# A decoder trunk on one core: its instructions ordered by the scheduler's timeline model in place of its default model

## The chip, the core and the metric

The kernel runs on one core of one Trainium2 chip. A core has five engines that each work through their own list of instructions in order: TensorE (PE in the profile, with weight loads shown as PEld), VectorE (DVE), ScalarE (ACT), GpSimd (POOL) and SyncE (SP). They meet only at semaphores. The metric is the device time of one execution in microseconds (us). The kernel before took 4318.94 us, the median of 3 runs (4314.97 to 4319.62).

## The reference

One layer of a hybrid decoder over 1024 tokens of width 1024, in float32:

```
h  = RMSNorm(x);  z = h @ W_in            # one projection, 77 tiles of 128 columns and 2 blocks for v
x += W_out( sum_b sigmoid(gate_b) * (mixer_b(z_b) @ P_b) )   # b: mLSTM, Mamba-2 SSD, forgetting attention
x += PEER(RMSNorm(x))
x += sigmoid(RMSNorm(x) @ W_g) * (p @ W_p);  out = RMSNorm(x)
```

PEER is the part that matters most here. For each token, 8 heads choose 16 experts each out of 16384 (two top-16 searches over 128 keys, then a top-16 of their sums). An expert is one row `u` and one row `v` of width 1024: `out = sum over the 128 chosen of softmax(score) * gelu(u . x) * v`.

## The kernel before

The tokens are split into two halves of 512, and each half into 4 blocks of 128 tokens. The stages, in the order in which the code is written and with the times that the trace shows (us):

- 0 to 1080: the mixer of half 0 (`mixer`), its output projection (`mixer_out`), and the expert search (`route_keys`: 16 projections, each followed by top-16 searches on DVE).
- 1080 to 1300: `route` of half 0, a chain of small DVE instructions for each of 4 blocks (top-16 at L891 to L895, selections at L933 to L943, the row numbers `ii` at L980). In between run the norm, the small per-head rows (`small_rows`, L355 to L443) and the first projections of the mixer of half 1.
- 1300 to 2330: the mixer of half 1. Beside it, `experts_in` fetches the 512 groups of `u` rows of half 0: POOL issues a gather of 128 rows (L1014, one row for each token, 512 KB), DVE multiplies them with the tokens and sums (L1027, a "row operation" in what follows). Five buffers hold gathered rows here, so POOL is at most five gathers ahead of DVE.
- 2330 to 2690: `mixer_out`, `route_keys` and `route` of half 1, and the first build of a weight table (below).
- 2690 to 4130: `experts_out`. The `v` rows are not gathered for the first 6 blocks. Instead the kernel reads the whole table `peer_v` and multiplies it with a table `W` of weights (token by expert, mostly zero). The 128 expert columns are taken in chunks of 43, 43 and 42, in two passes of three blocks: 6 chunks. For one column, SP loads 512 KB (`vr`, L1170, 4 buffers) and PE does 6 products that are two matmuls each in the trace (L1174, "a step" of 12 matmuls: 3 blocks by 2 halves of the width). While PE works through chunk n, the `W` of chunk n+1 is built by `scatter`: 48 times DVE makes one-hot tiles (`A8`, `B8` at L1091, two `A8` buffers, and the scaled `Bs` at L1103, two buffers), PE multiplies them (L1070, 24 small matmuls, "a small product") and ACT copies the result into `W` (L1072). The same loop feeds the row operations of half 1 (L1027, then L1044 for the last two blocks).
- 4130 to 4314: the gate of the per-layer input, the last norm, and the output.

All matmuls of the projections take weights split in two parts: SP loads `raw` (L191), ACT casts it to `whi` (L182), DVE forms `wlo` (L183), and PE does three matmuls for each of 8 slices (L214; L329 for the blocks of v). `raw`, `whi` and `wlo` have two buffers each.

The kernel is written with a tile framework. The code names the engine of every instruction; a scheduler then orders each engine's list. It plays the program through a model of the machine: whenever an engine of the model is free, it takes the earliest-written instruction that is ready in the model at that time. The order that results is fixed in the program; on the chip nothing is reordered. In `experts_out` DVE is exempt (its instructions stay as written); PE and ACT are not:

```
    with tc.manual_schedule(engines={mybir.EngineType.DVE}):
        end = experts_out(vp, W, blocks, gen, then, last())
```

## Time and profile before

| | |
|---|---|
| runs of the kernel (median of 3) | 4318.94 us |
| the profiled execution: time, span | 4315.76 us, 4314.0 us |
| PE busy | 3987.3 us, 92% of the span |
| DVE busy | 3297.0 us, 76% |
| POOL busy | 1726.7 us, 40% |
| ACT busy | 1179.5 us, 27% |
| data moved by DMA | 1018.30 MB, 236 GB/s over the span |

A share over the whole span mixes stages with different limits, so the stages are read one by one. Matmuls are pipelined: the durations of single matmuls overlap, and the busy time of a stretch is less than their sum.

### The profile page before, as it was taken

What the parts mean: (1) busy time and instruction counts of PE and PEld (TensorE: products, weight loads), DVE (VectorE), ACT (ScalarE), POOL (GpSimd) and SP (SyncE); (2) the same over time, 40 slices, a digit from 0 to 9 for tenths busy, and PEclk for the clock granted to TensorE, in tenths of its full rate; (3) what the DMA queues carried; (4) which work ended last, traced back from release to release, by engine and by line L of the source; (5) the groups of instructions that cost most, each with busy time, mean ns of one, the idle gap of its engine ahead of it and who ended that gap; (6) DMA issues with size and microseconds to landing.
All of it is one profiled execution on the core that took longest, in us unless ns stands there. A gap on an engine that the chain in (4) does not pass through costs nothing. (4 is left out here: it accounts for less than half of the span.)

```text
span 4314.0 us, 55488 instructions
## 1 busy us (share of the span) xinstructions
PE 3987.3 (92%) x20506; PEld 2494.4 (58%) x20506; DVE 3297.0 (76%) x6607; ACT 1179.5 (27%) x2194; POOL 1726.7 (40%) x1299
## 2 busy tenths in 40 slices
PE   8999999999788988989978798999999999998987
PEld 5777687777466755655744573544445444443455
DVE  6333245648998877788887799998899899997855
ACT  3343334533325502422521410211111111110023
POOL 0000000000036676565364001677777666777620
PEclk9999999999899997899989799999999999999998
DMA  2212122233258898788687124999999999999962
GB/s 91 99 56 76 46 93 71 77 126 122 78 173 296 299 355 291 276 310 313 217 298 282 59 96 149 335 357 361 369 364 376 364 358 361 358 376 400 399 222 93
DMA packets 326081, 1018.30 MB, mean 236 GB/s; under 512 B 33584, under 2 KB 81072, under 8 KB 325552
## 3 DMA queue, kind: packets, MB, share of 16 engines
q0 software_dynamic: 184320, 671.17, 42.6%
q1 hardware_dynamic: 141488, 343.58, 22.5%
q8 instruction: 161, 2.64, 0.2%
q14 instruction: 112, 0.92, 0.1%
HBM read 992.84 MB, written 21.77 MB: 235 GB/s over the span
## 5 line engine op out<-in xcount | busy, mean ns | idle before, releaser
L1014 POOL DMA_INDIRECT ug<-in_peer_u_dram,ii x1024 | 1397.3, 1365 | 2248.3 <-DVE ii L980 1388.6
L1174 PE MATMUL pair<-vr,W 128*128 128x512 f32 x3072 | 1388.7, 603 | 24.5 <-DMA vr<-in_peer_v_dram 24.5
L1027 DVE CUSTOM_DVE_ANT_0 ug<-ug,hft 128x1024 f32<-128x1024 f32 x1024 | 1217.8, 1219 | 158.8 <-DMA ug<-in_peer_u_dram,ii 142.5
L1174 PEld LDWEIGHTS pair<-vr,W 128*128 128x128 f32 x3072 | 569.3, 192 | 661.5 <-issue 633.9
L214 PE MATMUL bank<-hi,wlo 128*128 128x512 f32 x1552 | 623.3, 402 | 24.8 <-DVE wlo L183 24.6
L214 PE MATMUL bank<-hi,whi 128*128 128x512 f32 x1552 | 632.4, 409 | 12.0 <-ACT hi L182 5.1
L214 PE MATMUL bank<-lo,whi 128*128 128x512 f32 x1552 | 624.5, 403 | 0.9 <-DVE lo L183 0.8
L182 ACT CAST whi<-raw 128x1024 fp32r<-128x1024 f32 (+1 forms) x276 | 282.2, 1023 | 1070.9 <-PE bank L214 633.5
L183 DVE TENSOR_TENSOR wlo<-raw,whi 128x1024 fp32r<-128x1024 f32 (+1 forms) x276 | 327.1, 1186 | 323.2 <-ACT whi L182 312.6
L1072 ACT COPY W<-bank 128x176 f32<-128x176 f32 x480 | 179.9, 484 | 950.1 <-PE bank L1070 901.3
L1014 POOL DMA_INDIRECT ug<-in_peer_v_dram,ii x256 | 325.5, 1271 | 184.1 <-DVE hft L1044 95.0
L1044 DVE SCALAR_TENSOR_TENSOR hft<-ug,gt,hft 128x1024 f32<-128x1024 f32 x254 | 325.9, 1283 | 52.8 <-DMA ug<-in_peer_v_dram,ii 47.4
L214 PEld LDWEIGHTS bank<-hi,whi 128*128 128x128 f32 x1552 | 296.0, 191 | 105.3 <-issue 26.4
L214 PEld LDWEIGHTS bank<-hi,wlo 128*128 128x128 f32 x1552 | 296.2, 191 | 102.2 <-DVE wlo L183 32.9
L214 PEld LDWEIGHTS bank<-lo,whi 128*128 128x128 f32 x1552 | 296.4, 191 | 72.4 <-issue 9.7
L1070 PEld LDWEIGHTS <-A 128*128 128x128 bf16 x6912 | 215.2, 98 | 198.7 <-issue 80.9
L1091 DVE TENSOR_TENSOR A<-iota,i 128x1024 bf16<-128x1024 bf16 x288 | 197.4, 686 | 41.8 <-PE bank L1070 36.7
L205 PE MATMUL bank<-Y,raw 128*128 128x512 f32 x384 | 183.4, 636 | 27.8 <-DVE p L840 16.3
L1070 PE MATMUL bank<-Bs,A 128*128 128x43 bf16 (+1 forms) x5760 | 182.3, 183 | 22.4 <-DVE Bs L1103 21.7
L1103 DVE TENSOR_TENSOR Bs<-B,w 128x1032 bf16<-128x1032 bf16 (+1 forms) x288 | 198.4, 689 | 5.9
L205 PEld LDWEIGHTS bank<-Y,raw 128*128 128x128 f32 x384 | 76.6, 203 | 128.5 <-issue 90.3
L329 PE MATMUL pair<-whi,hi 128*128 128x512 f32 x256 | 102.7, 402 | 10.7 <-ACT mg L332 7.6
(429 smaller groups left out, 4492.4 us busy)
## 6 DMA issues: line engine op xcount, KB each, us to landing
vr<-in_peer_v_dram SPq DMA_DIRECT2D x256, 512.0 KB
raw<-in_w_in_dram SPq DMA_DIRECT2D x154, 512.0 KB
raw<-in_w_br_dram SPq DMA_DIRECT2D x64, 512.0 KB
raw<-in_w_tm_dram SPq DMA_DIRECT2D x32, 512.0 KB
raw<-in_w_q_dram SPq DMA_DIRECT2D x32, 512.0 KB
ug<-in_peer_u_dram,ii POOLq DMA_INDIRECT x1024
raw<-in_w_pg_dram SPq DMA_DIRECT2D x14, 512.0 KB
Y<-in_xT_dram SPq DMA_DIRECT2D x16, 256.0 KB
```

Source lines behind the costliest of these rows:

```text
L182: A.copy(out=hi, in_=src)
L183: V.tensor_tensor(out=lo, in0=src, in1=hi, op=ALU.subtract)
L205: PE.matmul(o, lhsT=raw[:, k, :], rhs=X[k] if isinstance(X, list) else X[:, k, :], start=k == 0, stop=k == nk - 1)
L214: PE.matmul(o, lhsT=l[:, k, :], rhs=r[k], start=i == 0, stop=i == n - 1)
L1014: G.indirect_dma_start(out=x, out_offset=None, in_=table, in_offset=bass.IndirectOffsetOnAxis(ap=ii[:, s:s + 1], axis=0))
L1027: V.tensor_tensor_reduce(out=ug, in0=ug, in1=hft, scale=1.0, scalar=0.0, op0=ALU.mult, op1=ALU.add, accum_out=act[:, s:s + 1])
L1044: V.scalar_tensor_tensor(out=o, in0=vg, scalar=gt[:, s:s + 1], in1=o, op0=ALU.mult, op1=ALU.add)
L1070: PE.matmul(wp_[:, u, 0:nk], lhsT=A8[:, a, :, o], rhs=Bs[:, k, a, :, o], start=k == 0, stop=k == 2)
L1072: A.copy(out=W[k][:, 0:hi - lo, b * P + t:b * P + t + 8].rearrange("p i t -> p t i"), in_=wp_[:, :, lo:hi])
L1091: V.tensor_tensor(out=o, in0=iota2[:, k0:k0 + n].unsqueeze(1).to_broadcast([P, 4, n, 2]), in1=x[:, t:t + 8].rearrange("p (a o) -> p a o", ...
L1103: V.tensor_tensor(out=Bs, in0=B8.unsqueeze(1).to_broadcast([P, 3, 4, nk, 2]), in1=w3[:, t // 8].rearrange("p k (a o) -> p k a o", o=2).uns ...
L1174: PE.matmul(acc[b][d], lhsT=l[:, b * P:b * P + P], rhs=raw[:, d * T:d * T + T], start=i2 == 0, stop=i2 == P - 1)
```

## The change

One argument where the framework's context is opened:

```
-    with tile.TileContext(nc) as tc:
+    with tile.TileContext(nc, schedule_with_timeline_sim=True) as tc:
         tile_trunk(tc, *aps, o)
```

The code that emits the instructions is untouched. The scheduler works with the same rule, but "free" and "ready" are now those of another model, its timeline model. The instructions are the same (17470 matmuls on PE, 1280 gathers on POOL, 819 plain DMAs on SP as the program counts them), but for the activation tables that ACT loads, 70 after 91, and for some instructions that only wait. Their order differs on all engines; on POOL and SP only by a few places.

On DVE, between two weight tiles `wlo` of the last v projection of half 1's attention (`proj_tm`, L329). `ug` is a buffer of gathered rows; the `L1027 ISA ug` rows are the row operations and `L1027 ISA act` their sums; `mg`, `p_pk`, `ii` belong to `route`, `pts`, `p4`, `cl` to `small_rows`, `rw` to the norm of q and k. Before, whole from the one `wlo` to the other but for the rows left out, 9 row operations and 8 others:

```order
L183 TENSOR_TENSOR wlo_1293_8782<-raw_1291_8779,whi_1292_8781 128x1024
L938 TENSOR_TENSOR mg_997_6549<-mg_997_6549 128x8x128
L1027 ISA ug_1944_13526,act_1925_13472<-ug_1944_13526,hft_1926_13473 128x1024
L1027 ISA act_1925_13472 128x1
L941 TENSOR_REDUCE p_pk_1244_8445<-mg_997_6549 128x128
...
L980 SCALAR_TENSOR_TENSOR ii_1245_8447<-p_pk_1241_8434,p_pk_1244_8445 128x128
...
L242 TENSOR_SCALAR rw_1283_8729<-rw_1283_8729 128x64
L183 TENSOR_TENSOR wlo_1296_8812<-raw_1294_8809,whi_1295_8811 128x1024
```

Now, the same two tiles and some of the 86 row operations and 112 others between them:

```order
L183 TENSOR_TENSOR wlo_1293_8782<-raw_1291_8779,whi_1292_8781 128x1024
L1027 ISA ug0_1990_13664,act_1925_13472<-ug0_1990_13664,hft_1926_13473 128x1024
L1027 ISA act_1925_13472 128x1
L933 TENSOR_TENSOR mg_997_6549<-p_pb_1213_8241,sta_11_128 128x2048
L987 RECIPROCAL p_gs_1220_8264<-p_gs_1220_8264 128x8
L1027 ISA ug1_1991_13667,act_1925_13472<-ug1_1991_13667,hft_1926_13473 128x1024
...
L980 SCALAR_TENSOR_TENSOR ii_1218_8259<-p_pk_1214_8246,p_pk_1217_8257 128x128
...
L265 TENSOR_SCALAR rw_1282_8727<-pair2_70 128x64
...
L241 TENSOR_TENSOR rw_1283_8729<-rw_1283_8729,rw_1284_8730 128x64
L183 TENSOR_TENSOR wlo_1296_8812<-raw_1294_8809,whi_1295_8811 128x1024
```

Row operations moved forward, from behind the tile to ahead of it, and `route` of the third and fourth block, which before stood mostly ahead of the first of the two tiles, moved back behind it. Counted from the first block's row numbers (`ii`, L980) to `wlo_1296`, 26 row operations stood there before and 149 stand there now. Ahead of `wlo_1293` it was 17 and is 63, ahead of the tile that DVE makes at 1868 us in the trace, 301 and 474. The last of the 512 stood in `mixer_out`; now it stands beside the output products of the mLSTM branch, ahead of the SSD mixer.

On PE, at the end of the third of the six builds of `W` (the one that ends at 3108.8 us in the trace; every row `L1070` shown is the first of the 24 of its small product, `Bs` names the product, `W_2803` is the table in use, `W_3069` the one being built). Before:

```order
L1070 MATMUL bank0_66<-Bs_3375_22402,A8_3369_22355 128x42
...
L1174 MATMUL pair0_68<-vr_3381_22443,W_2803_18264 128x512 x2
L1174 MATMUL pair1_69<-vr_3381_22443,W_2803_18264 128x512 x2
L1174 MATMUL pair2_70<-vr_3381_22443,W_2803_18264 128x512 x2
L1070 MATMUL bank1_67<-Bs_3382_22451,A8_3376_22404 128x42
...
L1174 MATMUL pair0_68<-vr_3388_22492,W_2803_18264 128x512 x2
L1174 MATMUL pair1_69<-vr_3388_22492,W_2803_18264 128x512 x2
L1174 MATMUL pair2_70<-vr_3388_22492,W_2803_18264 128x512 x2
```

Now, with nothing of L1174 between the rows shown:

```order
L1174 MATMUL pair1_69<-vr_3429_22751,W_3069_20299 128x512 x2
L1070 MATMUL bank1_67<-Bs_3339_22154,A8_3337_22124 128x42
...
L1070 MATMUL bank0_66<-Bs_3375_22402,A8_3369_22355 128x42
...
L1070 MATMUL bank1_67<-Bs_3382_22451,A8_3376_22404 128x42
...
L1070 MATMUL bank0_66<-Bs_3399_22581,A8_3397_22551 128x42
...
L1174 MATMUL pair2_70<-vr_3406_22623,W_3069_20299 128x512 x2
```

Steps of L1174 moved ahead of small products, so that a build begins with pairs of small products with two steps or so behind each pair, and ends with a run of small products that has no step in it. Of the 48 small products of a build, the last 24, 10, 13, 8 and 12 (second to sixth build) now have only 8, 0, 6, 0 and 0 products of L1174 among them (six products make a step; a build has some 150 of them in the second, some 250 in the later ones). Before, no more than two small products stood together without some of L1174 between them.

## Rows read from the trace of the kernel before

**Rows 1.** The page, part 1: engine, busy us, share of the span, instructions.
```profile
PE 3987.3 (92%) x20506; PEld 2494.4 (58%) x20506; DVE 3297.0 (76%) x6607; ACT 1179.5 (27%) x2194; POOL 1726.7 (40%) x1299
```
**Rows 2.** Stretch, us; busy us (count) of PE, PEld, DVE, ACT, POOL; clock, DMA, GB/s.
```profile
0.00:1090.00 1090.00, 1049.39 (x4824) 789.23 (x4824) 545.17 (x1288) 428.22 (x718) 3.92 (x19) 0.97 0.25 86
1090.00:1300.00 210.00, 168.32 (x624) 113.89 (x623) 206.99 (x578) 60.09 (x91) 45.76 (x32) 0.89 0.40 132
...
1295.00:1868.00 573.00, 504.97 (x2255) 344.76 (x2254) 462.05 (x799) 212.54 (x362) 358.07 (x277) 0.90 0.86 301
1868.00:2330.00 462.00, 412.10 (x1572) 264.43 (x1571) 378.92 (x626) 120.58 (x195) 263.00 (x202) 0.95 0.84 293
2330.00:2455.00 125.00, 92.95 (x1252) 58.85 (x1251) 104.82 (x199) 48.27 (x120) 5.73 (x5) 0.76 0.28 101
```
**Rows 3.** Costliest groups: line, engine, operation, tiles, count | busy us, mean ns | idle before.
```profile
L1174 PE MATMUL pair<-vr,W 128*128 128x512 f32 x3072 | 1388.7, 603 | 24.5 <-DMA vr<-in_peer_v_dram 24.5
L1027 DVE CUSTOM_DVE_ANT_0 ug<-ug,hft 128x1024 f32<-128x1024 f32 x1024 | 1217.8, 1219 | 158.8 <-DMA ug<-in_peer_u_dram,ii 142.5
...
L1027 DVE DVE_READ_ACCUMULATOR2_ANT act<- 128x1 f32 x1024 | 82.7, 81 | 0.0
```
**Rows 4.** Time line of DVE at the two tiles of the change.
```profile
1278.14 1.22 DVE L183 TENSOR_TENSOR wlo<-raw,whi 128x1024 fp32r<-128x1024 f32 x1
...
1295.09 1.22 DVE L183 TENSOR_TENSOR wlo<-raw,whi 128x1024 fp32r<-128x1024 f32 x1
```
**Rows 5.** Instructions of L1027 alone in the same stretches (two for each row operation).
```profile
1180.00:1295.00 115.00, 31.59 (x52) 0.92 0.55 178
1295.00:1868.00 573.00, 332.99 (x552) 0.90 0.86 301
1868.00:2330.00 462.00, 243.35 (x403) 0.95 0.84 293
```
**Rows 6.** Waits: engine and line, waited for: us in total, times, longest.
```profile
DVE ug L1027 <- DMA ug<-in_peer_u_dram,ii: 142.5, 146, 3.6
...
PE pair L1174 <- DMA vr<-in_peer_v_dram: 24.5, 5, 16.0
```
**Rows 7.** Busy time by engine in the stretches of the six builds.
```profile
2349.00:2442.00 93.00, 70.93 (x1192) 47.67 (x1192) 85.07 (x160) 41.05 (x106) 0.00 (x0) 0.76 0.17 55
2686.00:2851.00 165.00, 162.73 (x1406) 83.41 (x1403) 162.44 (x300) 35.89 (x96) 116.79 (x80) 1.00 0.94 336
2866.00:3109.00 243.00, 239.28 (x1586) 119.33 (x1585) 220.61 (x402) 36.06 (x98) 186.48 (x131) 0.99 0.98 369
3126.00:3361.00 235.00, 233.02 (x1575) 116.67 (x1574) 216.43 (x396) 37.17 (x99) 179.63 (x126) 1.00 0.98 370
3379.00:3636.00 257.00, 246.88 (x1604) 122.30 (x1603) 236.03 (x299) 37.79 (x103) 170.67 (x134) 0.98 0.98 369
3653.00:3893.00 240.00, 238.58 (x1595) 119.19 (x1594) 219.16 (x388) 35.45 (x98) 179.49 (x127) 1.00 0.97 366
```
**Rows 8.** L1070 alone in the third build (24 matmuls for each small product).
```profile
2866.00:3109.00 243.00, 34.56 (x1104) 33.76 (x1104) 0.99 0.98 369
```
**Rows 9.** The gathers: duration ns least/median/most, first and last start.
```profile
L1014 POOL DMA_INDIRECT ug<-in_peer_u_dram,ii x1024: 932/1277/2925, 1133.3 to 3900.8; - x171
```
**Rows 10.** Time line of PE, one small product and one step.
```profile
2864.60 0.76 PE L1070 MATMUL bank<-Bs,A 128*128 128x42 bf16 x24
2865.20 5.40 PE L1174 MATMUL pair<-vr,W 128*128 128x512 f32 x12
```
**Rows 11.** Time line of PE after a wait of 7.59 us.
```profile
1284.64 0.80 PE L329 MATMUL pair<-whi,hi 128*128 128x512 f32 x1 [7.59 <-ACT mg L332]
...
1289.06 0.63 PE L329 MATMUL pair<-wlo,hi 128*128 128x512 f32 x1
...
1290.55 0.39 PE L329 MATMUL pair<-whi,lo 128*128 128x512 f32 x1
```

## The prediction

> **What bounds the kernel now.** I read the page's busy shares first, then the stretches stage by stage, then the time line at the places where the order changes, and the waits last. PE is busy for 3987 of 4314 us [rows 1], so the whole kernel has 327 us in which PE stands still, and a new order can win at most a part of them. The stretches show who holds PE up. From 0 to 1090 us PE works 1049 of 1090 us and DVE half the time: PE's own. From 1090 to 1300 DVE works 207 of 210 us and PE 168: DVE's. From 1295 to 2330 both are loaded, PE with 505 of 573 and 412 of 462 us, DVE with 462 and 379. From 2330 to 2455 DVE is full again (105 of 125) and PE is not (93) [rows 2]. In the builds of W, 2686 to 3893, everything is loaded at once: in the third build PE works 239 of 243 us, DVE 221, and the DMA engines are at 0.98 [rows 7]. There the order in which PE and DVE hand work to each other decides, since neither has room to catch up.
>
> **First term: row operations ahead of the weight tile.** A row operation costs DVE 1219 + 81 ns, 1.30 us [rows 3]. Before, 26 of them run before wlo_1296: the stretch from 1180 to 1295 us has 52 instructions of L1027, two for each [rows 5], and 1295.09 us is where that tile's subtraction starts [rows 4]. Now 149 stand ahead of it, 123 more, and 123 x 1.30 = 160 us. DVE was full up to there (207 of 210 us, [rows 2]), so at most 3 us of this fit into idle time: the tile comes 157 us later. PE cannot go on without it: between the tiles before and this one PE has a few matmuls of 0.4 us each (0.39 us a matmul at full clock, [rows 11]), and DVE has 86 row operations (112 us) and 112 other instructions that used to lie ahead of the first tile. The gathers keep up: the first starts at 1133.3 us [rows 9], and 149 row operations in 1295 - 1133 + 157 = 319 us are one in 2.1 us, the pace that was held from 1295 to 1868 us beside the mixer (573/276, 552 instructions, [rows 5]).
>
> What comes after pays some back and adds some. Up to the place that PE reached at 1868 us, 301 row operations stood before and 474 stand now: of the 173 more, 123 are counted, 50 remain, 65 us of DVE. The stretch has 573 - 462 = 111 us of idle DVE and 573 - 505 = 68 us of idle PE [rows 2]. Bounds: all 65 us vanish into DVE's idle time (0), or none does (+65). I take +50, near the upper end, because the idle time is waits of DVE for PE, ACT or gathers (146 waits of 0.98 us on gathers over the kernel, [rows 6]) that a fuller DVE list does not remove. From 1868 to 2330 us, 201 row operations ran (403 instructions, [rows 5]) and 38 are left, so DVE is no longer in the way and PE alone counts: it worked 412 of 462 us [rows 2]. Bounds: 0 to -50, I take -25. In the last stretch, 2330 to 2455, the first build of W ran between the last row operations and the products of mixer_out; the build's own 93 us [rows 7] and some 7 us of norm stay, the other 25 us can go: 0 to -30, I take -25. Sum of the term: 157 + 50 - 25 - 25 = +157 us, bounds 157 - 80 = 77 and 157 + 65 = 222.
>
> **Second term: runs of small products without a step.** A small product takes PE 34.56 us / 46 = 0.75 us (1104 matmuls, 24 each, [rows 8]) and a step 5.4 us, 0.90 us for each of its six products [rows 10]. For each small product DVE makes two one-hot tiles and Bs and does the row operations that stand between: its busy time in a build over 46 small products is 162.4/46 = 3.53 us in the second, then 4.80, 4.71, 5.13 and 4.76 us [rows 7]. Before, each small product has about a step beside it, 0.75 + 5.4 = 6.2 us of PE against 4.8 us of DVE, so PE never waits long. Now PE uses up the steps early and a run of n small products is left. DVE cannot have made them beforehand: A8 and Bs have two buffers, so DVE is one product ahead when the run begins and PE gets the others at DVE's pace, n - 1 times. Second build: 23 x 3.53 = 81 us, less PE's work in the run, 24 x 0.75 + 8 x 0.90 = 25: PE idles 56 us. Third: 9 x 4.80 - 10 x 0.75 = 36. Fourth: 12 x 4.71 - 13 x 0.75 - 6 x 0.90 = 41. Fifth: 7 x 5.13 - 6 = 30. Sixth: 11 x 4.76 - 9 = 43. Sum +206 us. The rest of each build is PE-bound, as before, with the same matmuls in it: PE had 1 to 10 us to spare in each [rows 7], so nothing is won there. The chunk's end is a true barrier: W is complete only with the last small product, and PE can run ahead by the four vr buffers alone. Bounds: if DVE is two ahead, one product less in each of five runs, -23 us, 183; if in the runs the gathers set the pace, 131 row gathers in 243 us or 1.86 us each, 2.85 for each small product, 5.3 us instead of 4.8, 62 times +0.5, 237.
>
> **Small terms.** A run leaves PE nearly idle, and PE comes back slow: after a wait of 7.59 us the matmuls follow each other at 0.43 us and take 0.63, until 1289.5 us, then 0.39 [rows 11], half the clock (1.2 GHz, then 2.4) for 4.9 us, 2.4 us lost. In the first build, small products alone with little beside them, the granted clock was 0.76 [rows 7]. Six returns cost 15 us; bounds 0 and 25. After a run, four vr buffers come free at once and are loaded again beside the gathers; PE waited for vr 24.5 us in 5 waits over the kernel, up to 16 us [rows 6]. Five more such places: 0 to 5 x 5 us, I take +15. On the page TensorE: Matmul & The Clock Gate, Part 1, the Trainium skill says the same of a PE that has stood idle, that it starts again at half rate and must be busy for a while; by it the price would be of the same order and the sum would not change. The 21 activation tables fewer are ACT's, whose lists lag nowhere behind PE's and DVE's in the stretches named (60 busy of 210 us, 213 of 573, 121 of 462, [rows 2]): 0. From 0 to 1080 us and from 4130 us on, the lists differ by single places; bounds -10 and +10, I take 0.
>
> **Sum.** The profiled execution took 4315.76 us, 3.2 below the median of the runs. 4315.8 + 157 + 206 + 15 + 15 = 4709, and I predict 4705 us. With all lower bounds 4316 + 77 + 183 - 10 = 4566, with all upper ones 4316 + 222 + 237 + 25 + 25 + 10 = 4835.
>
> **Rivals.**
> 1. The runs of small products are hidden: DVE gets far enough ahead while PE works through the pairs of steps, for instance because ACT and DVE run ahead in what does not need A8. Then only the first term is left, 4316 + 157 + 15 = 4488. For it: before, DVE idles 22 of 243 us in a build. Against it: two buffers, and DVE's list as written.
> 2. The front-loaded rows are paid back in full: from 1868 us on, DVE has 163 row operations less (212 us) and all of PE's 50 + 32 us idle time goes, and the stretch to 1868 adds nothing. Then 4316 + 157 - 82 + 206 + 30 = 4627 with the runs as they are; this lies inside the forecast's range.
> 3. Worse: DVE's lists are now so dense that every row operation waits for its gather at the pace of 2.1 us, in the mixer too: 325 row operations from wlo_1296 to the place of 1868 us at 2.1 us are 683 us against 573 + 50, 60 us more, and the runs at their upper bound: 4705 + 60 + 31 + 20 = 4815 to 4870.
> 4. Faster: the early row operations use DMA time that lay idle (0.40 from 1090 to 1300, [rows 2]) and free DVE later, so that from 1295 to 2455 PE has no wait left: 68 + 50 + 32 = 150 us won. It decides at wlo_1296: only if that tile comes less than 150 us late does it win, and if the runs of small products cost nothing besides. With a tile 120 us late and PE gapless behind it, 4316 + 120 - 150 = 4286.
> 5. The order does not matter, since the busiest engine sets the time: its matmuls are the same, 4316. The Trainium skill (Trace Analysis, Identifying the Most-Contended Engine) says to find the engine of highest occupancy and to improve that; by it alone the time would be about 4316. The trace disagrees in two stretches, 1090 to 1300 and 2330 to 2455, where PE waits for a full DVE [rows 2].
>
> **How the numbers follow.** Forecast with its bounds, rival 2 within it (4566 to 4835): 0.74. Rival 1: 0.09. Rival 3 above 4835: 0.07, below it counts above. An order in between, one of the terms at half its size (4500 to 4566): 0.05. Rival 4: 0.03. Rival 5: 0.02. A measurement of this kernel can tell 0.2%, 9 us, from no change. Faster is rival 4: 0.03; same is rival 5: 0.02; slower all others: 0.95. From 4500 to 4830 about 8 in 10 lie: the forecast but for its upper end, and the orders in between.
>
> **What would show it.** In the profile after: a stretch of 130 us or more behind 1290 us in which PE does nearly nothing and DVE alternates row operations with route and small_rows; the first 512 row operations done 200 us or so before the mixer ends; in each of the five later builds a stretch of 56, 36, 41, 30 and 43 us with only L1070 on PE, a granted clock below 1 there, and waits of PE on Bs or A8 of 200 us in all. PE's busy time stays near 3987 us and its share falls to 85%. The prediction is wrong if PE has no such gap at wlo_1296, if PE's waits for Bs stay below 100 us, or if the time is under 4500 us.

## The result and the profile after

The changed kernel takes 4814.57 us (median of 4 runs, 4806.32 to 4818.2) against 4319.28 us for the kernel before (4314.97 to 4321.75): a ratio of 1.115, 95% interval 1.1137 to 1.1166, 495 us slower. Forecast were 4705 us, 4500 to 4830.

The page, part 1, answers to [rows 1]:

```profile
PE 4039.5 (84%) x20506; PEld 2552.0 (53%) x20506; DVE 3301.1 (69%) x6607; ACT 1147.1 (24%) x2173; POOL 1768.3 (37%) x1299
```

The work is the same. PE's 52 us more are the same matmuls at a lower clock (0.893 granted on the mean, 0.949 before). The span is 4815.4 us, so PE stands still for 776 us, where it was 327. Next the stretches of [rows 2], between the same places of PE's work (the third begins at the place that PE reached at 1300 us, not at 1295; stretch; busy us and count of PE, PEld, DVE, ACT, POOL; granted clock; DMA share; GB/s):

```profile
0.00:1145.00 1145.00, 1066.97 (x4822) 801.32 (x4823) 536.31 (x1248) 415.48 (x708) 3.71 (x19) 0.94 0.24 82
1145.00:1527.00 382.00, 171.39 (x625) 116.11 (x624) 354.11 (x863) 62.27 (x93) 242.97 (x154) 0.72 0.71 242
1527.00:2162.00 635.00, 519.22 (x2237) 349.77 (x2236) 513.91 (x887) 205.72 (x357) 424.13 (x322) 0.84 0.88 309
2162.00:2590.00 428.00, 401.58 (x1598) 264.29 (x1597) 207.37 (x318) 116.33 (x192) 50.70 (x37) 0.97 0.33 117
2590.00:2725.00 135.00, 93.62 (x1222) 64.14 (x1221) 88.38 (x164) 45.37 (x112) 0.00 (x0) 0.67 0.18 56
```

The second stretch took 210 us and takes 382, with PE busy for 171 us as before (168). One hole, a stretch in which PE does nothing at all, makes most of the difference. In this window of it DVE is busy for 147 of 165 us:

```profile
1340.00:1505.00 165.00, 0.00 (x0) 0.00 (x0) 147.14 (x304) 5.51 (x10) 126.58 (x79) 0.51 0.74 251
```

What ends it is in the time line of PE, and of ACT (start, us; in brackets the idle time before and what ended it):

```profile
1506.63 0.79 PE L329 MATMUL pair<-whi,hi 128*128 128x512 f32 x1 [166.73 <-ACT mg L332]
```

```profile
1480.50 0.31 ACT L1030 ACTIVATE act<-act 128x128 f32<-128x128 f32 x1 [28.34 <-DVE act L1027]
1505.02 2.05 ACT L332 COPY mg<-pair 128x512 f32<-128x512 f32 x4 [24.21 <-DVE p_pk L941]
```

PE waits for ACT to empty the accumulators of the v projection (L332). ACT copies them into `mg`, and `mg` is still in use: `route` keeps its scratch there (`ge`, `gm`), until the last selection of the fourth block (L941) has run on DVE. And DVE is late because row operations stand between the small instructions of `route` and `small_rows`: 78 of them (92 of DVE's 147 us) beside 149 other instructions in the window above. In places they alternate one for one:

```profile
1441.15 0.20 DVE L894 MAX8 p_ts<-mg 128x8 f32<-128x50 f32 x1
1441.27 1.21 DVE L1027 CUSTOM_DVE_ANT_0 ug<-ug,hft 128x1024 f32<-128x1024 f32 x1
1442.40 0.08 DVE L1027 DVE_READ_ACCUMULATOR2_ANT act<- 128x1 f32 x1
1442.40 0.21 DVE L894 MAX8 p_ts<-mg 128x8 f32<-128x50 f32 x1
1442.53 1.21 DVE L1027 CUSTOM_DVE_ANT_0 ug<-ug,hft 128x1024 f32<-128x1024 f32 x1
```

The weight tile of the forecast, `wlo_1296`, comes just as late. DVE makes it here:

```profile
1524.55 1.23 DVE L183 TENSOR_TENSOR wlo<-raw,whi 128x1024 fp32r<-128x1024 f32 x1 [1.03 <-ACT whi L182]
```

After the hole PE has 48 matmuls to do before the group of 24 that needs this tile. That group starts at 1526.19 us; the tile is ready at 1525.78.

The five later builds of W, to be held against [rows 7]. From their first to their last small product they took 173, 250, 242, 264 and 247 us before (the stretches in [rows 7] start some 7 us inside them) and take 230, 281, 282, 299 and 306 us now, so each is 31 to 59 us longer. The granted clock, 0.98 to 1.00 there before, is 0.83 to 0.93:

```profile
2950.00:3180.00 230.00, 175.66 (x1459) 96.12 (x1456) 170.95 (x314) 35.55 (x101) 114.64 (x84) 0.83 0.71 241
3190.00:3471.00 281.00, 249.03 (x1646) 126.28 (x1641) 222.38 (x406) 35.59 (x102) 188.43 (x131) 0.93 0.90 323
3480.00:3762.00 282.00, 239.51 (x1610) 122.34 (x1609) 224.17 (x408) 37.11 (x104) 187.96 (x132) 0.90 0.91 326
3773.00:4072.00 299.00, 263.73 (x1689) 133.58 (x1686) 242.11 (x310) 38.15 (x105) 176.35 (x138) 0.93 0.89 325
4081.00:4387.00 306.00, 253.73 (x1664) 128.85 (x1661) 224.50 (x394) 35.24 (x101) 181.47 (x129) 0.91 0.86 308
```

The end of the third build on PE's time line. The first two rows are how most of the build looks, some two steps and then a pair of small products; the run begins with the fourth row:

```profile
3411.35 13.12 PE L1174 MATMUL pair<-vr,W 128*128 128x512 f32 x30
3424.31 1.37 PE L1070 MATMUL bank<-Bs,A 128*128 128x42 bf16 x48
3425.51 3.68 PE L1174 MATMUL pair<-vr,W 128*128 128x512 f32 x8
3429.03 0.76 PE L1070 MATMUL bank<-Bs,A 128*128 128x42 bf16 x24
3431.82 0.78 PE L1070 MATMUL bank<-Bs,A 128*128 128x42 bf16 x24 [2.02 <-DVE Bs L1103]
3436.82 1.02 PE L1070 MATMUL bank<-Bs,A 128*128 128x42 bf16 x24 [4.22 <-DVE Bs L1103]
3441.82 1.02 PE L1070 MATMUL bank<-Bs,A 128*128 128x42 bf16 x24 [3.98 <-DVE Bs L1103]
```

One small product comes each 5.0 us, and PE waits for about 4 of them; the first two take 0.76 and 0.78 us, the others 1.02, since the clock has fallen (0.60 from 3425 to 3471 us, where DVE is busy for 45.7 of 46 us). The waits, for [rows 6] (engine and line, waited for: us in total, times, longest):

```profile
PE bank L1070 <- DVE Bs L1103: 185.3, 55, 6.2
PE pair L329 <- ACT mg L332: 166.7, 1, 166.7
DVE A L1091 <- PE bank L1070: 238.7, 65, 9.9
DVE ug L1027 <- DMA ug<-in_peer_u_dram,ii: 130.7, 143, 3.9
PE pair L1174 <- DMA vr<-in_peer_v_dram: 26.0, 7, 12.3
PE bank L214 <- ACT ug L182: 25.9, 1, 25.9
```

The first and the third were before:

```profile
PE bank L1070 <- DVE Bs L1103: 21.7, 15, 9.8
DVE A L1091 <- PE bank L1070: 36.7, 17, 4.2
```

The first, and the second, which was 7.6 us ([rows 11]), belong to the two terms of the forecast. The third is the other face of the first: while PE works through the steps between two pairs of small products DVE waits for it, and does not make up for that later.

A third loss was not forecast. In the mixer of half 0 PE reaches the end of `route_keys` at 1145.5 us, 55 us later than before, with no row operation anywhere near. PE's time line there has a chain of small matmuls with nothing between its links:

```profile
575.59 0.41 PE L252 MATMUL pair<-ident,tmp 8*128 8x8 f32 x4
576.32 0.41 PE L252 MATMUL pair<-ident,tmp 8*128 8x8 f32 x4 [0.32 <-ACT tmp L249]
579.81 0.60 PE L259 MATMUL pair<-ident,rw 128*8 128x128 f32 x4 [3.08 <-DVE rw L682]
583.38 2.67 PE L270 MATMUL pair<-rn,eye 96*128 96x512 bf16 x5 [2.97 <-DVE rn L226]
586.72 1.25 PE L270 MATMUL pair<-rn,eye 96*128 96x512 bf16 x2 [0.67 <-DVE Y L696]
591.16 0.59 PE L270 MATMUL pair<-rn,eye 96*128 96x512 bf16 x1 [3.19 <-DVE Y L696]
```

Before, the same eight matmuls of L270 lay between projections, up to 24 matmuls of L214 to one of them, and PE waited for none (in the time line of before):

```profile
549.47 0.39 PE L214 MATMUL bank<-hi,wlo 128*128 128x512 f32 x1
549.70 0.39 PE L270 MATMUL pair<-rn,eye 96*128 96x512 bf16 x1
549.74 0.59 PE L214 MATMUL bank<-hi,whi 128*128 128x512 f32 x1
...
555.39 0.39 PE L270 MATMUL pair<-rn,eye 96*128 96x512 bf16 x1
```

The spans of the two profiled executions differ by 501 us. Where the start of the same matmul is compared in both traces, 497 of them are these: 55 in half 0, 172 at the hole, 67 from there to the place of 1868 us, -35 to 2330, +12 to 2455, -4 up to the second build, 222 in the five builds, -28 from the last build to the end of the steps, +36 behind it.

### The profile page after: what moved, and what is told of

It is laid out like the page before. It is cut to its first block, busy times and chain, and to the rows that moved or that the text cites. A ratio compares the mean times of both kernels' runs of the same rounds, so it can differ in the third digit from the quotient of the medians.

```text
span 4815.4 us, 55447 instructions
## 1 busy us (share of the span) xinstructions
PE 4039.5 (84%) x20506; PEld 2552.0 (53%) x20506; DVE 3301.1 (69%) x6607; ACT 1147.1 (24%) x2173; POOL 1768.3 (37%) x1299
## 5 line engine op out<-in xcount | busy, mean ns | idle before, releaser
L1014 POOL DMA_INDIRECT ug<-in_peer_u_dram,ii x1024 | 1443.7, 1410 | 2670.8 <-DVE ii L980 1824.8
L1174 PE MATMUL pair<-vr,W 128*128 128x512 f32 x3072 | 1371.2, 604 | 32.4 <-DMA vr<-in_peer_v_dram 26.0
L1027 DVE CUSTOM_DVE_ANT_0 ug<-ug,hft 128x1024 f32<-128x1024 f32 x1024 | 1216.2, 1219 | 150.0 <-DMA ug<-in_peer_u_dram,ii 130.7
L1174 PEld LDWEIGHTS pair<-vr,W 128*128 128x128 f32 x3072 | 582.7, 193 | 728.3 <-issue 692.2
L214 PE MATMUL bank<-hi,whi 128*128 128x512 f32 x1552 | 628.5, 407 | 17.9 <-ACT hi L182 6.8
L214 PE MATMUL bank<-lo,whi 128*128 128x512 f32 x1552 | 616.2, 397 | 7.1 <-DVE lo L183 7.1
L214 PE MATMUL bank<-hi,wlo 128*128 128x512 f32 x1552 | 615.5, 397 | 5.2 <-DVE wlo L183 4.7
L1070 PEld LDWEIGHTS <-A 128*128 128x128 bf16 x6912 | 223.7, 103 | 295.5 <-DVE Bs L1103 189.3
L1091 DVE TENSOR_TENSOR A<-iota,i 128x1024 bf16<-128x1024 bf16 x288 | 197.8, 687 | 252.2 <-PE bank L1070 238.7
L214 PEld LDWEIGHTS bank<-hi,whi 128*128 128x128 f32 x1552 | 295.2, 191 | 123.8 <-issue 28.7
L1070 PE MATMUL bank<-Bs,A 128*128 128x43 bf16 (+1 forms) x5760 | 187.1, 188 | 186.2 <-DVE Bs L1103 185.3
L214 PEld LDWEIGHTS bank<-lo,whi 128*128 128x128 f32 x1552 | 295.8, 191 | 78.0 <-DVE lo L183 11.0
L214 PEld LDWEIGHTS bank<-hi,wlo 128*128 128x128 f32 x1552 | 295.1, 190 | 76.6 <-DVE wlo L183 11.2
L329 PE MATMUL pair<-whi,hi 128*128 128x512 f32 x256 | 105.8, 413 | 173.3 <-ACT mg L332 166.7
L1103 DVE TENSOR_TENSOR Bs<-B,w 128x1032 bf16<-128x1032 bf16 (+1 forms) x288 | 198.4, 689 | 5.3
L205 PE MATMUL bank<-Y,raw 128*128 128x512 f32 x384 | 169.6, 598 | 7.4 <-DMA raw<-in_w_br_dram 5.6
L329 PEld LDWEIGHTS pair<-whi,hi 128*128 128x128 f32 x256 | 50.8, 198 | 191.6 <-ACT mg L332 167.2
```

What stands on the lines that cost most here:

```text
L205: PE.matmul(o, lhsT=raw[:, k, :], rhs=X[k] if isinstance(X, list) else X[:, k, :], start=k == 0, stop=k == nk - 1)
L214: PE.matmul(o, lhsT=l[:, k, :], rhs=r[k], start=i == 0, stop=i == n - 1)
L1014: G.indirect_dma_start(out=x, out_offset=None, in_=table, in_offset=bass.IndirectOffsetOnAxis(ap=ii[:, s:s + 1], axis=0))
L1027: V.tensor_tensor_reduce(out=ug, in0=ug, in1=hft, scale=1.0, scalar=0.0, op0=ALU.mult, op1=ALU.add, accum_out=act[:, s:s + 1])
L1070: PE.matmul(wp_[:, u, 0:nk], lhsT=A8[:, a, :, o], rhs=Bs[:, k, a, :, o], start=k == 0, stop=k == 2)
L1091: V.tensor_tensor(out=o, in0=iota2[:, k0:k0 + n].unsqueeze(1).to_broadcast([P, 4, n, 2]), in1=x[:, t:t + 8].rearrange("p (a o) -> p a o", ...
```

## The experiments

Three theories stand against each other. Mine: two places in the order, each with its own price, that add. Rival A: the price is DVE's and the gathers' denser list, whatever PE's order. Rival B: row operations done early are paid back later, so that holding them gives little. All runs are compared with the 4815 us after and with the kernel before, whose median was 4313 to 4319 us beside the different runs.

**PE as written in experts_out**, under the timeline model:

```
-    with tc.manual_schedule(engines={mybir.EngineType.DVE}):
+    with tc.manual_schedule(engines={mybir.EngineType.DVE, mybir.EngineType.PE}):
```

> Timeline model everywhere, but in experts_out PE keeps the order of the code, as DVE does already. Theory (runs of small products): the five later builds come back from 230, 281, 282, 299 and 306 us to 173, 250, 242, 264 and 247 us, within 6 us each, PE's waits on Bs fall from 185 to under 40 us; the steps that PE had saved up for the end (209 us after the last build, 237 before the change) are given back, so 4815 - 222 + 28 = 4620 us, 4590 to 4640. Rival (the builds are long because DVE and the gathers got denser, whatever PE's order): less than 60 us won, 4755 or more. The gap of 167 us at 1340 us stays as it is by both.

Measured: 4642.53 us (1.0757 of before, 1.0731 to 1.0784), 172 us won, 2.5 us beyond the range's upper end. The five builds take 184, 255, 245, 269 and 256 us, the first and last of them further off than the 6 us that I gave. The hole is there, and the wait for Bs mostly gone, though not under 40 us:

```profile
PE pair L329 <- ACT mg L332: 166.1, 1, 166.1
PE bank L1070 <- DVE Bs L1103: 49.6, 30, 11.9
```

Rival A falls: DVE's list in `experts_out` is the written one, as in the changed kernel, and the builds are short.

**The control**: the same edit in the kernel before.

> The kernel before (default model) with PE in the order of the code in experts_out: the control for the first run. Theory: the default model's order is nearly the written one there, 4319 us, 4305 to 4335. Rival: the written order is itself better than the default's, under 4300, and then the first run's gain is not all a repair of runs of small products; or it is worse by over 20 us, then that gain is understated.

Measured: 4345.01 us (1.0052, 1.0029 to 1.0076), 27 us more than before (13 to 33 by the interval), so the expected range was missed. PE's waits for Bs are twice those of before:

```profile
PE bank L1070 <- DVE Bs L1103: 44.6, 30, 11.5
```

The written order is itself that much worse than the default model's, and in the same place: the five builds take 1203 us together, 1175 before, 1398 in the changed kernel and 1209 with PE as written under the timeline model. So the 172 us understate the repair: 172 + 27 = 199 us for the runs of small products.

**Row operations held back**, under the timeline model. The 17th row operation and those behind it read `hft`, and one element of `hft` is written again (plus zero times the last row numbers) once `route` is done:

```
         for s, ug in rows(peer_u, ii, extra):
+            if after is not None and s == 16:
+                V.scalar_tensor_tensor(out=hft[:, 0:1], in0=after, scalar=0.0,
+                                       in1=hft[:, 0:1], op0=ALU.mult, op1=ALU.add)
...
+                           r0[3][1][:, 0:1] if tb == 0 else None):
```

> Timeline model everywhere, but the row operations of half 0 from the 17th on depend on the last row numbers (ii) of route, so the scheduler cannot put them between route's instructions; 29 of them stand ahead of wlo_1296 now, 151 in the changed kernel, 26 in the one before. PE's order in experts_out is that of the changed kernel. Theory (route, and behind it the mixer, is late by the row operations between its instructions): the 167 us gap of PE at 1340 us falls under 20 us; of the later parts +67 stays up to the place of 1868 us (363 rows ahead of it, 477 and 301 in the other two) and the 35 us won behind it become some 13, so 4815 - 167 + 22 = 4670 us, 4640 to 4700. Rival (the rows have to be done anyway beside the mixer, so holding them only moves the cost): less than 80 us won, over 4735.

Measured: 4733.57 us (1.0969, 1.0942 to 1.0995), 81 us won, not 145. The hole is gone: PE's longest wait there is 13.0 us, and behind it PE is 68 us late (55 of them from half 0) in place of 227. But 78 us come back. Up to the place of 1868 us it loses 76 us (67 in the changed kernel), and up to that of 2330 another 35, where the changed kernel wins 35: the row operations now meet the state-space scan of half 1, in which a chain of small matmuls waits for small instructions of DVE and ACT. DVE's stand between row operations: in the window below 56 row operations are 68 of its 92 us:

```profile
2200.00:2300.00 100.00, 58.51 (x225) 36.41 (x224) 92.07 (x158) 22.15 (x50) 76.58 (x57) 0.69 0.89 307
```

In the changed kernel the last row operation is done at 2240 us, and the same chain, later in time, finds DVE without them (207 of 428 us busy from 2162 to 2590 us). So rival B is half right: the hole was an advance payment for about half of its length.

**Both edits:**

> Timeline model with both edits of the other two runs. Theory: the two costs lie in different stretches and add, 4815 - 195 - 145 = 4475 us, 4445 to 4505; what is left over the kernel before (about 155 us) is the mixer of half 0 (55), the part from 1300 to 1868 us (67) and the last stage (36). Rival (both edits uncover the same limit, DVE's 3300 us of work): the gains overlap by more than 50 us, over 4525.

Measured: 4563.49 us (1.0571, 1.0545 to 1.0596), 251 us won, and 172 + 81 = 253: the two add, as they should if they lie in different stretches. The time misses my range because each part alone was smaller than expected (172 us for 195, 81 for 145), not because the gains overlap.

**Runs of small products by themselves**, in the kernel before with PE as written (the control): the steps of builds 3 to 6 are emitted LEAD iterations ahead of the small products beside them.

```
+                early = LEAD if 0 < n < len(chunks) - 1 else 0
+                for i_ in (range(early + 1) if i == 0 else [i + early] if i + early < nk else []):
...
-        ex = [(vp, f"ug{i}") for i in range(5)]
+        ex = [(vp, f"ug{i}") for i in range(4)]
```

> Default model, PE in written order in experts_out as in the control of 4345 us, but in four of the six chunks the steps are written 4 iterations ahead of the small products, so that builds 3 to 6 end with 7 small products without a step between them (2 in the control); one gather buffer fewer (7 for 8) to make room. Theory (a run of n small products costs (n - 1) x 4.85 us of DVE less n x 0.75 us of PE): 23.9 for n = 7 against 3.4 for n = 2, 20.5 us more in each of 4 builds, 4345 + 82 = 4427 us, 4400 to 4455. Rival (DVE uses the steps at the start of the chunk to get ahead, the run is hidden): within 25 us of 4345.

> The same with the steps 10 iterations ahead: runs of 13 or 14 small products in four builds. Theory: 12.5 x 4.85 - 13.5 x 0.75 = 50.5 us, 47 more than in the control, 4345 + 4 x 47 = 4534 us, 4500 to 4570, so some 106 us above the kernel with 4. Rival (hidden): under 4400.

Measured: 4412.73 us (1.0232, 1.0202 to 1.0262) with 4 and 4533.13 us (1.0510, 1.0484 to 1.0536) with 10. Over the control that is 68 and 188 us, where the formula gives 82 and 189; from 4 to 10, two kernels with the same number of gather buffers, it is 120 us against 106. PE's waits for Bs were 44.6 us in the control; here they are, first with 4 and then with 10 (a line is added above, so that L1070 and L1103 are L1071 and L1104):

```profile
PE bank L1071 <- DVE Bs L1104: 111.5, 52, 11.9
```

```profile
PE bank L1071 <- DVE Bs L1104: 215.0, 79, 12.0
```

So runs of small products cost this without the timeline model too. The sum, (n - 1) times DVE's time for a product less PE's own, counts PE's waits, and these grew by 67 and 170 us, four fifths to nine tenths of it. With 10 the other 18 us of the 188 are something else, and that the two totals agree to 1 us is partly luck.

**Three buffers for A8 and Bs** in the kernel with 10:

```
-BB = 2
+BB = 3
...
-                A8 = ab[t // 8 % 2].tile([P, 4, P, 2], BF, tag="A8", name=nm("A8"), bufs=1)
+                turn["a"] = (turn.get("a", 0) + 1) % 3
+                A8 = ab[min(turn["a"], 1)].tile([P, 4, P, 2], BF, tag="A8", name=nm("A8"), ...
```

> The kernel with the steps 10 iterations ahead, with three buffers for A8 and for Bs in place of two. Theory (DVE can be ahead by the buffers, so one product fewer of each run is made at DVE's pace): 4.85 us less in each of 4 builds, 19 us, 10 to 25 below the kernel with two. Rival (something else holds DVE at a run's start, such as ACT's copies or the one B8 buffer): within 6 us of the kernel with two.

Measured: 4526.80 us (4525.25 to 4536.92), 6 us less, with the runs of both kernels overlapping: no gain that can be told, and not the 10 us at least that I expected. In the 108 us ahead of a run DVE waited for PE only 2.2 us in the kernel with two buffers, and was busy for 98.7: it was at its own pace already, which would leave a third buffer nothing to hold. In the changed kernel DVE does wait for PE (238.7 us); whether more buffers would help there was not tried, and the two buffers as a cause of n - 1 stay unproved.

**The dot products of half 0 left out**, under both models, the gathers kept, to see what remains from 1260 us on without row operations. The scheduler orders each of the two kernels anew.

```
-            V.tensor_tensor_reduce(out=ug, in0=ug, in1=hft, ..., accum_out=act[:, s:s + 1])
+            if extra[0][1] == "ug0" and len(extra) == 2:        # half 0
+                V.tensor_tensor(out=act[:, s:s + 1], in0=ug[:, 0:1], in1=hft[:, 0:1], op=ALU.mult)
...
```

> Timeline model, row operations of half 0 replaced by one product of 128x1 (some 0.06 us in place of 1.30), gathers as they are: leaves out the dot products of half 0. Theory (from 1260 to 2330 us the change costs through DVE's row operations): the gap of 167 us at 1340 us falls under 30 us, and at the end of the mixer of half 1 the kernel is some 60 to 110 us behind the default model's kernel with the same cut, of which 55 is there already at 1080 us. Rival (from 1260 on PE's own order costs as in half 0, rows or not): 150 us or more behind at that place.

> Default model with the same cut as the run before (dot products of half 0 left out): its reference. That run took 4541 us, stands 52 us behind the kernel before at 1200 us and level with it at the end of the mixer of half 1. Theory (rows or not, both models differ by what PE's own order costs in half 0, and by little from there on, if DVE has few row operations): the default model's kernel gains 40 to 70 us by the cut between 1260 and 2330 us, 4318 - 55 = 4263 us, 4240 to 4280. Rival (PE's order costs in the mixer of half 1 too, about as in half 0): it gains 100 us or more, under 4220.

Measured: 4540.51 us under the timeline model and 4169.04 us under the default one. (The product of 128x1 takes 0.15 us in the trace, not 0.06.) The first half of my expectation holds, since the hole is gone: from 1150 to 1700 us no wait of PE is longer than 9.6 us. The second fails: the default model gains 144 us by the cut, not 55, and the rival has it. The first matmul of `mixer_out` of half 1 tells how late the mixer ends; four rows of the view of L205 (durations ns, first and last start), in the order before, after, without dot products under the timeline model, and without them under the default one:

```profile
L205 PE MATMUL bank<-mg,raw x128: 592/592/1202, 2313.0 to 2397.2; 128*128 128x512 f32 x128
```

```profile
L205 PE MATMUL bank<-mg,raw x128: 592/592/676, 2573.5 to 2632.1; 128*128 128x512 f32 x128
```

```profile
L205 PE MATMUL bank<-mg,raw x128: 592/592/676, 2303.2 to 2361.9; 128*128 128x512 f32 x128
```

```profile
L205 PE MATMUL bank<-mg,raw x128: 592/592/676, 2198.6 to 2283.0; 128*128 128x512 f32 x128
```

With rows the mixer of half 1 ends 2573.5 - 2313.0 = 260 us late, without them 2303.2 - 2198.6 = 105. Half 0 is 55 and 57 of that. So of 205 us lost between, 157 hang on row operations. The other 48 are lost with hardly any of them: the rest of the order makes them, and whether it is PE's, DVE's or ACT's was not told apart.

**Half 0 by itself**: the first part (mixer of half 0 to `route_keys`) in a block of its own, ordered by either model, all behind it by the default one.

```
-        H, c = mixer_head(0)
-        k0 = route_keys(0, mixer_out(0, mixer(0, H, c)))
+        with tc.block(schedule_with_timeline_sim=True):      # or tc.block()
+            H, c = mixer_head(0)
+            k0 = route_keys(0, mixer_out(0, mixer(0, H, c)))
```

> Default model, the first part (mixer of half 0, its output projection and route_keys, up to 1080 us) in a block of its own, so that it is ordered by itself: the reference of the next run. Both theories: the price of the block's end, at which the engines meet, 4318 + 10 to 60 us.

> The same block, ordered by the timeline model; all behind it by the default model. Theory (the 55 us that the changed kernel lags at 1080 us come from PE's order in the mixer of half 0: the projections that cover the chains of small matmuls are used up early): 45 to 65 us over the kernel with the default block. Rival (they come from work of half 1 that the scheduler draws forward into half 0): within 15 us of it.

Measured: 4321.13 us with the default block (1.0014, 0.9999 to 1.003: the block's end costs nothing that can be told, less than expected) and 4388.91 us with the timeline one (1.0156, 1.012 to 1.0192), 68 us apart, 3 us more than the range. In the traces `route_keys` ends at 1085.2 and 1137.5 us, 52 us apart, as in the changed kernel. So half 0's loss is made inside half 0, by the order there and not by work drawn forward from half 1. The block orders all engines, so that it does not tell PE's part from theirs. The other 16 to 28 us come behind the block, where the two lists differ in some places too; they were not followed up.

**PE of half 0 as written**, in the kernel with both edits; there hardly a projection stands between the links:

```
-        k0 = route_keys(0, mixer_out(0, mixer(0, H, c)))
+        with tc.manual_schedule(engines={mybir.EngineType.PE}):
+            k0 = route_keys(0, mixer_out(0, mixer(0, H, c)))
```

> The kernel with both edits (timeline model, 4563 us), and PE in half 0 in the order of the code, in which nearly no projection stands between the chains of small matmuls. Theory (a chain of small matmuls without a projection between its links is paid in full): half 0, 57 us behind the kernel before in the run with both edits, falls behind by 120 to 250 us, 4563 + 65 to 195, so 4630 to 4760 us. Rival (the chains cost the same wherever they stand): within 25 us of 4563.

Measured: 4827.51 us (1.1166, 1.1123 to 1.1208), 264 us over the kernel with both edits, beyond the 195 that I allowed. `route_keys` ends at 1430.1 us, 283 later. PE's stretch up to there, first in the kernel with both edits (end at 1147.5 us), then in this one:

```profile
0.00:1147.00 1147.00, 1069.88 (x4821) 802.97 (x4822) 536.37 (x1248) 415.52 (x708) 3.69 (x19) 0.94 0.25 82
```

```profile
0.00:1430.00 1430.00, 1179.89 (x4824) 863.39 (x4824) 552.10 (x1288) 434.29 (x720) 3.71 (x19) 0.86 0.20 65
```

The same 4824 matmuls take 1180 us of PE for 1070, at a granted clock of 0.86, and PE stands still for 250 us, not 77. Busy time times the granted clock of the stretch is 1006 and 1015 us, nearly the same work. So two fifths of the price (110 of 283 us) are the clock, the rest waits. No version with all its row operations beats the kernel before.

## Why the prediction was right or wrong, point by point

- **Second term, runs of small products, +206 us: right in mechanism and size.** PE's idle time in the five builds, from the first small product to the last, is 53.9, 31.7, 42.5, 35.3 and 52.3 us, forecast 56, 36, 41, 30 and 43. In sum 216 us for 206; less the 20 us that PE idled there before, the change is 196. Taking the order back wins 199, and runs made by hand cost 170 us of waits where the same formula gives 189. Why DVE is only one product ahead, the two buffers by my account, stays unproved. With the small terms beside it (15 for the clock, 15 for vr) I had 236 us, and the builds grew by 222. Vr's part was wrong (26.0 us of waits, 24.5 before); the 222 - 196 = 26 us that are no idle time are PE's own work at a lower clock.
- **First term, its first step, +157 us at the weight tile: the size is nearly right, the link that ends the wait is another.** PE stands still for 166.7 us and is 172 us further behind. What it waits for is not `wlo_1296`, which DVE forms only at 1524.55 us, behind the end of the wait, but the buffer `mg`, which `route` gives back late. That the size came out so near is partly luck: the two stand close together in DVE's list, behind nearly the same row operations, so that the count of 123 served for either. The step "PE cannot go on without it" was still sound. The tile came 174 us late beyond half 0's 55 (1524.55 - 1295.09 - 55), and PE reached the group that uses it 0.4 us after it was ready. With `mg` given back early and the row operations left where they are, PE would by DVE's list have got 48 matmuls further and stood at the tile until about 1525 us; this was not run.
- **The steps behind it: +50, -25, -25.** Measured +67, -35 and +12. The first is 2 us beyond my bound of 65, the second inside. The third failed with its reason. Before, 24 of the first 47 small products of the first build had matmuls of `mixer_out` behind them; now 6 have, and the other 41 run by themselves. The 47 take 127 us from the first to the last, 92 before. The term as a whole is 216 us for 157, 6 us below its upper bound of 222.
- **What I put down to row operations is not all theirs.** The runs without dot products show 48 of the 205 us lost in the mixer of half 1 with hardly any row operation on DVE. And holding the rows wins 81 us, not 145, since the held rows meet another chain later.
- **"From 0 to 1080 us and from 4130 us on, the lists differ by single places; bounds -10 and +10": this step failed.** Half 0 lost 55 us. The lists do not differ by single places there: matched by line and tile in the two traces, matmuls of L214 stand up to 146 places earlier in PE's order of half 0 and small matmuls up to 120 places later. Projections moved away from a chain leave its links bare: 68 matmuls of L214 in a row at 482 to 498 us are followed by 28 us of small matmuls, 2.9 us of it waits, at a granted clock of 0.66 (498 to 522 us). PE's lag is 5 us at the place of 450 us before, 34 at 550 and 55 at 850, the stretch of the mLSTM's and the SSD's chains. That the order inside half 0 makes it is shown, which engine's is not. At the end, PE needs 28 us less from the last build to the end of the steps and loses 36 us behind them, most of it in one wait of 25.9 us for `ug`, a buffer of the last row sums.
- **The sum.** I had 393 us, the list above has 497. Of the 104 missing, 55 are half 0, 37 the stretch with the first build, 15 the first step (172 for 157), 17 the one behind it, 8 the end; -10 (1868 to 2330), -14 (the five builds) and -4 came out better than forecast. The time is 110 us above the 4705 and 15 us below the top of the range, 4830: of half 0's 55 us no more than 10 were in any bound, and that the range held is partly luck.
- **Rivals.** That the runs are hidden (4488) fell with PE's 185 us of waits for Bs. That the rows are paid back in full (4627) did not come true in the changed kernel, but it describes half of what holding them brings. That each row operation waits at the gathers' pace (4815 to 4870) gives the measured time, at its lower end, for a wrong reason: DVE's waits for gathers fell from 142.5 to 130.7 us. That the order is faster (4286) needed a tile less than 150 us late; it came 174 us late. That the order does not matter, since the busiest engine sets the time (4316), fell too: PE's matmuls and their count are the same here, and the time is 11.5% longer. The Trainium skill (Perfetto Trace Analysis, Identifying the Most-Contended Engine) says to improve the engine of highest occupancy first. PE is that engine before and after (92% and 84%), so by this case the rule names the engine; that its work sets the time was the rival's own step.

## What to carry to other kernels

An order is priced by what it leaves uncovered: on each engine look for chains of short dependent instructions (top-16 searches, scans, one-hot products) and ask which independent work lies between their links before and after. A run of n bare products cost here about n - 1 times the producer's time for one, less the consumer's own (216 us of waits for 206, and 170 for 189 in the runs made by hand), and that was worked out from a trace before anything was run. Where a long filler instruction shares a list with such a chain, follow every tile and buffer that the chain releases: the wait appears at the one that is needed first, and the next may stand close behind it.

## What the runs showed that was not expected

A bare chain costs not only its waits: with PE of half 0 as written, 110 of 283 us are the same matmuls made slower at a granted clock of 0.86. In the runs of small products, with PE busy for 14 of 46 us, it falls to the lower of the two levels of its clock (a small product takes 1.02 us for 0.76; 0.60 granted on the mean from 3425 to 3471 us, and 0.52 from 3111 to 3163 us of the kernel with 10 steps ahead). A block of its own for the first quarter of the kernel cost some 6 us or nothing (1.0014, 0.9999 to 1.003).
